# A two-layer encoder with expert retrieval: u blocks and gathered rows respaced, routing casts on ScalarE, gate scratch in groups of four blocks

## The chip, the core and the metric

One NeuronCore of a Trainium2 chip runs the whole kernel as one program. The metric is the device time of one execution in microseconds (us), lower being better. Engines are named as in the profile: PE is TensorE (matmuls; PEld its weight loads), DVE VectorE, ACT ScalarE, POOL GpSimd, SP SyncE, whose queue issues most loads.

## What is computed

Two residual layers over 512 tokens of width 1024: a mixer (convolution and windowed attention, or dense attention and spatial gating), then a retrieval layer over 16384 experts, and a last RMSNorm. The change lies in the retrieval layer alone:

```python
q = (ht @ wq).reshape(T, PEER_HEADS, 2, PEER_DKEY // 2)
s = jnp.einsum('thpd,hpkd->thpk', q, subkeys.astype(q.dtype)).astype(jnp.float32)
sv, si = lax.top_k(s, PEER_TOPK)
cand = (sv[:, :, 0, :, None] + sv[:, :, 1, None, :]).reshape(T, PEER_HEADS, PEER_TOPK * PEER_TOPK)
fv, fi = lax.top_k(cand, PEER_TOPK)
i1 = jnp.take_along_axis(si[:, :, 0, :], fi // PEER_TOPK, axis=-1)
i2 = jnp.take_along_axis(si[:, :, 1, :], fi % PEER_TOPK, axis=-1)
eidx = i1 * PEER_NKEYS + i2
gate = jax.nn.softmax(fv, axis=-1)
# for every token, over its 8 x 16 experts e: out += gelu(u[e] . x) * gate * v[e]
```

## The kernel before

The experts of a layer are 128 blocks of 128. For three of the four token tiles (384 tokens) the retrieval is done densely: a **u block** multiplies one block of `u` with all 384 tokens (24 matmuls `up` in three-term fp32r), ACT applies gelu (`A`), the result is multiplied with a gate matrix that is zero where an expert was not chosen, and a v block multiplies that with `v`. The fourth tile (GT) is done by gathering: a **row** is one gathered row of `u` or `v` per token (indirect DMA on POOL, tile `ug`) and one product on DVE; 256 rows per layer.

A u block takes a step of `u_step` (L1002): load of block b+3 on SP (`ur`, three buffers), rounding `uh` on ACT and remainder `ul` on DVE of block b+1 (two buffers each), gelu of the block before, matmuls of block b. While the routing is under way a block is **parked**: `A` is written to DRAM (`Ad`) and read back later (`Ar`). Blocks that are left when the routing ends are **fresh** and go straight into the combined stage of u and v blocks.

The routing is DVE's work: `topk` (L1101) finds the 16 best keys per head and half (an item is ten instructions for two halves), `route_top` (L1109) the 16 best sums, `route_rest` (L1227) the key numbers, by one-hot products and a `tree` of additions (L1206). `g_prep` and `g_build` (L1302, L1314) make one-hot matrices per token, PE multiplies them into the gate matrix (`gp`), ACT copies that to `stg`, and 12 writes of 2 MB per layer put it into DRAM scratch `Gd` (L1294); the combined stage reads it back as `G`, one read for four blocks (L1419).

All engines run in the order in which the program names their instructions; there is no scheduler. What sets the spacing is `tick` (L1044): each piece of routing work reports a cost in about microseconds of DVE, every `row_every` of it a row is put in, and every `u_every` (rows included at 1.15) a u block:

```python
            u_every, row_every = st["pace"]
            if st["rows"] and st["row"] < 2 * P:
                st["racc"] += cost
                while st["racc"] >= row_every and st["row"] < 2 * P:
                    st["racc"] -= row_every
                    row()
                    cost += 1.15
            st["acc"] += cost
            while st["acc"] >= u_every:
                st["acc"] -= u_every
                u_step()
```

PACE_T holds in the searches, PACE_R in the routes, PACE_G in the one-hot builds. Ahead of these stages stands the query loop (L1188), nine turns of query products, score products `sps`, and searches of tile GT and tile 0.

Of the kernel before, what the change touches and what calls it, by code (L numbers as in the profile page):

```python
# [10 lines left out]
F32 = mybir.dt.float32  # L11
# [9 lines left out]
P = 128  # L21
# [37 lines left out]
URB = 3  # L59
RAW1 = 2  # L60
RAWX = 8
AU = (8,)
LAST = 3
DGA = 3
F0 = 6
# [1 line left out]
AFILL = 2  # L67
QFILL = (2, 1)
CFILL = (3, 5, 4, 2)
PACE_T = (3.5, 3.7)  # L70
PACE_R = (3.5, 3.0)
PACE_G = (3.5, 3.0)
GSC = 4096.0
CSTART = [0, 16, 24, 29, 33, 36, 38, 40] + list(range(42, 50))
# [6 lines left out]
def trunk(ctx: ExitStack, tc: tile.TileContext, a: dict, out: bass.AP, stages=99):  # L81
# [3 lines left out]
    def pool(name, side):  # L85
        return tc.tile_pool(name=name, bufs=1, side=side, reuse_waits="tile")
# [864 lines left out]
    def peer(l, A, B):  # L951
# [2 lines left out]
        TG = ND * 4  # L954
        GT = NT - 1
        base = l * NK * NK
        Gd = tc.dram_tile([TG, P, NK, 32], F32, name=f"Gd{l}")
        Ad = [tc.dram_tile([P, SD], F32, name=f"Ad{l}_{b}") for b in range(NB)]
        ea, eb = ExitStack(), ExitStack()
        up = ea.enter_context(pool(f"ua{l}", A))  # L960
# [83 lines left out]
        def tick(cost):  # L1044
            if not st["pace"]:
                return
# [3 lines that stand above are left out]
                while st["racc"] >= row_every and st["row"] < 2 * P:  # L1050
                    st["racc"] -= row_every
                    row()
                    cost += 1.15
            st["acc"] += cost
            while st["acc"] >= u_every:
                st["acc"] -= u_every
                u_step()
# [43 lines left out]
        def topk(h, t, wkp):  # L1101
            xs = [2 * h, 2 * h + 1]
            srcs = [Ss[h][p][:, t, :] for p in range(2)]
            wks = [wkp.tile([P, NK], F32, tag="wk", bufs=4, name="wk") for _ in range(2)]
            top16(zip(xs, srcs, wks), sv[t], si[t])

        tops = {}

        def route_top(t, h0, h1, mid=None):  # L1109

            if t not in tops:
                tops[t] = [pl["a"].tile([P, NH, 16], dt, tag="f" + x, bufs=1, name="f" + x)
                           for x, dt in (("v", F32), ("i", U32))]
            hs, n = slice(h0, h1), h1 - h0
            c5 = pl["a"].tile([P, NH, NC50], F32, tag="c5", bufs=1, name="c5")[:, hs]
            v4 = sv[t].rearrange("p (h s) j -> p h s j", s=2)[:, hs]
            for j in range(8):
                m = 16 // (j + 1)
                nc.vector.tensor_tensor(c5[:, :, CSTART[j]:CSTART[j] + m], v4[:, :, 1, :m],
                                        v4[:, :, 0, j:j + 1].to_broadcast([P, n, m]), OP.add)  # L1120
            nc.vector.tensor_tensor(c5[:, :, 42:50], v4[:, :, 0, 8:16],
                                    v4[:, :, 1, 0:1].to_broadcast([P, n, 8]), OP.add)
            tick(1.2)
            if mid:
                mid()
            for h in range(0, n, 2):
                top16([(h0 + h + j, c5[:, h + j, :], pl["a"].tile([P, NC50], F32, tag="wk2", bufs=4, name="wk2"))
                       for j in range(2)], *tops[t])
                tick(1.25)

        pl["a"] = cs_.enter_context(pool(f"a3{l}", A))
        with pool(f"rq{l}", A) as qp:
            wraw, wspl, sps, qs = {}, {}, {}, {}

# [53 lines left out]
            for h in range(NH + 1):  # L1188
                w_load(h + 2)
                if h < NH:  # L1190
                    q_mm(h)
                if h:
                    s_mm(h - 1)
                    s_copy(h - 1)
                if h < NH:
                    q_split(h)
                w_split(h + 2)
                if h:
                    topk(h - 1, GT, qp)
                if h and h % RSTEP == 0:  # L1200
                    route_top(GT, h - RSTEP, h)
                elif h > 1:
                    topk(h - 2, 0, qp)
                if h in AU:
                    u_step()
        def tree(ms, extra=()):  # L1206
            extra = list(extra)
            n = 16
# [18 lines left out]
        def route_rest(t):  # L1227
# [8 lines left out]
            sf = pl["r"].tile([P, 2, 16, NH], F16, tag="sf", bufs=2, name="sf")  # L1236
            nc.vector.tensor_copy(sf.rearrange("p s j h -> p h s j"), si[t].rearrange("p (h s) j -> p h s j", s=2))
            dl = pl["r"].tile([P, 2, 16, NH], F16, tag="dl", bufs=2, name="dl")
            nc.vector.tensor_copy(dl[:, :, 0:1, :], sf[:, :, 0:1, :])
            nc.vector.tensor_sub(dl[:, :, 1:, :], sf[:, :, 1:, :], sf[:, :, :15, :])  # L1240
            fkf = fk.rearrange("p k h -> p (k h)")
            tick(1.3)

            def jkh(x):
                return x.rearrange("p j (k h) -> p j k h", h=NH)
# [4 lines left out]
            def oh(name):  # L1250
# [5 lines left out]
            nc.vector.tensor_tensor(jkh(m), jkh(ge), tab(dl[:, 0]), OP.mult)  # L1256
            m2 = oh("mk2")
            nc.vector.tensor_tensor(jkh(m2), jkh(ge), tab(diffT), OP.mult)
            tick(3.4)
            i1, sa = tree([m, m2])  # L1260
            bb = pl["r"].tile([P, 16, NH], F16, tag="bb", bufs=2, name="bb")
            nc.vector.tensor_sub(bb.rearrange("p k h -> p (k h)"), fkf, sa)
            nc.vector.tensor_copy(gt[:, 0].rearrange("p k h -> p (k h)"), i1)
            tick(2.6)
            ge2 = oh("ge2")
            nc.vector.tensor_tensor(jkh(ge2), bb[:, None].to_broadcast([P, 16, 16, NH]), tab(jT), OP.is_ge)
            m = oh("mk")
            nc.vector.tensor_tensor(jkh(m), jkh(ge2), tab(dl[:, 1]), OP.mult)
            gsum = sm.tile([P, NH], F32, tag="gsum", name="gsum")
            nc.vector.tensor_reduce(gsum, ga, AX.X, OP.add)  # L1270
            tick(3.5)
            i2 = tree([m], [lambda: nc.vector.reciprocal(gsum, gsum)])[0]
            nc.vector.tensor_copy(gt[:, 1].rearrange("p k h -> p (k h)"), i2)
            nc.vector.tensor_tensor(gt[:, 2].rearrange("p k h -> p h k"), ga,
                                    gsum.unsqueeze(2).to_broadcast([P, NH, 16]), OP.mult)
            tick(2.5)
            return gt.rearrange("p x k h -> p x (k h)")

        gq = []
# [1 line left out]
        def g_flush():  # L1281
            t, s, A2, Bh, Bl, stg = gq.pop(0)
            o = 16 * (s % 2)
            for q in range(4):
                gp = bank("v", [P, 4, NK], name="gp")
                for j in range(4):
                    tt = 4 * q + j
                    w, n = tt // TI, tt % TI
                    nc.tensor.matmul(gp[:, j, :], A2[:, w, :, n], Bh[:, w, :, n], start=True, stop=False)  # L1289
                    nc.tensor.matmul(gp[:, j, :], A2[:, w, :, n], Bl[:, w, :, n], start=False, stop=True)  # L1290
                nc.scalar.activation(stg[:, :, o + 4 * q:o + 4 * q + 4], gp.rearrange("p t i -> p i t"), AF.Copy,  # L1291
                                     scale=1.0 / GSC)
            if s % 2 == 1:
                nc.gpsimd.dma_start(Gd[t * 4 + s // 2], stg)  # L1294

        def g_transpose(gt):
            tp = bank("m", [P, 3, P], name="gtp")
# [1 line left out]
                nc.tensor.transpose(tp[:, j, :], gt[:, j, :], ident)  # L1299
            return tp  # L1300

        def g_prep(tp):  # L1302
            iT = pl["r"].tile([P, 2, P], F16, tag="iT", bufs=2, name="iT")
            nc.vector.tensor_copy(iT, tp[:, 0:2, :])
            g32 = pl["r"].tile([P, P], F32, tag="g32", bufs=2, name="g32")
            nc.vector.tensor_scalar(g32, tp[:, 2, :], GSC, None, OP.mult)
            gg = pl["r"].tile([P, 2, P], F16, tag="gg", bufs=2, name="gg")
            nc.vector.tensor_copy(gg[:, 0, :], g32)
            nc.vector.tensor_sub(gg[:, 1, :], g32, gg[:, 0, :])
            nc.vector.tensor_copy(g32, gg[:, 1, :])  # L1310
            tick(1.0)
            return iT, gg, g32

        def g_build(t, iT, gg, g32):  # L1314
# [45 lines left out]
                row_load()  # L1360

        def mid():
            hold["tp"] = g_transpose(hold["gt"])

        with pool(f"o3{l}", A) as pl["r"]:
            pl["oh"] = 3
# [13 lines left out]
        pl["r"] = pl["a"] = rt.enter_context(pool(f"ro{l}", A))  # L1380
# [31 lines left out]
        def v_load(i):  # L1412
# [242 lines left out]
```

## Time and profile before

| | us |
|---|---|
| median of 3 runs (lowest to highest) | 2888.75 (2886.06 to 2889.57) |
| the profiled execution | 2888.71 |
| its span, first to last instruction | 2886.6 |
| PE busy / DVE / ACT / POOL | 2788.8 / 2355.8 / 1220.9 / 765.8 |

In a layer the stages follow each other: the mixer, the query loop, the routing with its u blocks (layer 0 from 303 us, layer 1 from 1734), the combined stage (from 771 and 2199 us). PE's busy time counts matmuls in flight; the granted clock of a stretch is a share of 2.4 GHz, where time at the lower level counts as a half.

### The profile page before, as it was taken

Reading aid. Unit: us, or ns where it says so; the run is one execution under the profiler, and the core shown is the slowest. Engines: PE = TensorE matmul, PEld = TensorE weight load, DVE = VectorE, ACT = ScalarE, POOL = GpSimd, SP = SyncE. Lnnn points to the kernel's source line nnn. Section 1 sums busy time; section 2 is a strip of 40 time slices with the busy share of each in tenths; the row PEclk is TensorE's granted clock in tenths of the full one; section 3 lists DMA queues with packets and bytes.
Section 4 is the critical chain, followed back from the end, with each engine's and each line's share of the span. In section 5 each row is a group of like instructions: output and inputs, shape, how many; then the busy total and the mean of one; then the engine's idle time right before and its main releaser. Section 6 shows DMA issues by size and latency. Waiting matters only on the chain.

```text
span 2886.6 us, 43523 instructions
## 1 busy us (share of the span) xinstructions
PE 2788.8 (97%) x15844; PEld 2510.2 (87%) x15844; DVE 2355.8 (82%) x4692; ACT 1220.9 (42%) x2139; POOL 765.8 (27%) x730
## 2 busy tenths in 40 slices
PE   8999899999999999999999998899999999999998
PEld 7888789999999998888799888898999999888886
DVE  7866999888788887878777479998887888788887
ACT  4664324555533333333356333344564333333333
POOL 0000243333344442222100002343333444322220
PEclk9999999999999999999999999999999999999999
DMA  5102467889999999999812125677999999999995
GB/s 152 59 23 93 149 225 241 302 300 332 357 346 337 333 335 345 345 347 344 287 56 79 41 85 193 227 263 276 322 336 359 348 345 343 312 352 339 354 344 202
DMA packets 334343, 752.39 MB, mean 261 GB/s; under 512 B 27888, under 2 KB 184944, under 8 KB 331056
## 3 DMA queue, kind: packets, MB, share of 16 engines
q1 hardware_dynamic: 245424, 395.41, 40.5%
q0 software_dynamic: 88704, 354.20, 33.9%
q8 instruction: 124, 2.03, 0.3%
q14 instruction: 91, 0.75, 0.1%
HBM read 661.69 MB, written 87.82 MB: 260 GB/s over the span
## 4 chain that ended last, share of the span: by engine, by line
PE 79%; DVE 16%; ACT 2%; issue 2%; DMA 1%; SPq 0%; ACTq 0%; DVEq 0%
PE va L148 11%; PE va L146 11%; PE va L147 11%; PE up L148 9%; PE up L146 9%; PE up L147 9%; DVE ul L143 3%; DVE ug L1027 2%; PE gp L1289 1%; PE gp L1290 1%; PE O L417 1%; PE qp L146 1%; PE qp L147 1%; PE qp L148 1%; DVE wk L1064 1%
## 5 line engine op out<-in xcount | busy, mean ns | idle before, releaser
L148 PE MATMUL up<-hh,ul 128*128 128x384 f32 x2048 | 702.0, 343 | 46.5 <-DVE ul L143 46.3
L146 PE MATMUL up<-hh,uh 128*128 128x384 f32 x2048 | 702.2, 343 | 6.1 <-ACT A L990 5.6
L147 PE MATMUL up<-hl,uh 128*128 128x384 f32 x2048 | 696.8, 340 | 0.8 <-DVE hl L143 0.8
L146 PE MATMUL va<-vh,Wh 128*128 128x512 f32 x1536 | 600.7, 391 | 7.1 <-ACT Wh L1439 7.1
L148 PE MATMUL va<-vh,Wl 128*128 128x512 f32 x1536 | 600.3, 391 | 0.0
L147 PE MATMUL va<-vl,Wh 128*128 128x512 f32 x1536 | 599.3, 390 | 0.0
L142 ACT CAST uh<-ur 128x1024 fp32r<-128x1024 f32 x256 | 268.7, 1050 | 595.2 <-PE up L147 564.8
L1017 POOL DMA_INDIRECT ug<-in_peer_un,idx x256 | 354.3, 1384 | 614.9 <-DVE ug L1027 556.7
L1017 POOL DMA_INDIRECT ug<-in_peer_v,idx x256 | 296.4, 1158 | 680.8 <-DVE gacc L1036 633.4
L1438 ACT CAST vh<-vr 128x1024 fp32r<-128x1024 f32 x256 | 268.6, 1049 | 443.6 <-issue 283.3
L148 PEld LDWEIGHTS up<-hh,ul 128*128 128x128 f32 x2048 | 389.3, 190 | 61.8 <-DVE ul L143 61.5
L143 DVE TENSOR_TENSOR ul<-ur,uh 128x1024 fp32r<-128x1024 f32 x256 | 313.3, 1224 | 151.5 <-ACT uh L142 151.3
L1442 DVE TENSOR_TENSOR vl<-vr,vh 128x1024 fp32r<-128x1024 f32 x256 | 312.9, 1222 | 130.9 <-ACT vh L1438 130.7
L146 PEld LDWEIGHTS up<-hh,uh 128*128 128x128 f32 x2048 | 389.2, 190 | 11.8 <-ACT A L990 7.9
L147 PEld LDWEIGHTS up<-hl,uh 128*128 128x128 f32 x2048 | 389.1, 190 | 4.5 <-DVE hl L143 1.3
L146 PEld LDWEIGHTS va<-vh,Wh 128*128 128x128 f32 x1536 | 289.2, 188 | 65.1 <-ACT Wh L1439 7.9
L148 PEld LDWEIGHTS va<-vh,Wl 128*128 128x128 f32 x1536 | 289.1, 188 | 61.9 <-DVE Wl L1443 0.8
L147 PEld LDWEIGHTS va<-vl,Wh 128*128 128x128 f32 x1536 | 289.3, 188 | 59.0 <-DVE vl L1442 0.6
L1036 DVE SCALAR_TENSOR_TENSOR gacc<-ug,ag,gacc 128x1024 f32<-128x1024 f32 x254 | 325.2, 1280 | 3.9 <-DMA ug<-in_peer_v,idx 1.6
L1027 DVE SCALAR_TENSOR_TENSOR ug<-ug,hrow 128x1024 f32<-128x1024 f32 x256 | 306.0, 1218 | 0.0
L992 POOL DMA_DIRECT2D Ad<-A x180 | 101.6, 565 | 722.7 <-ACT A L990 720.7
L1291 ACT ACTIVATE stg<-gp 128x512 f32<-128x512 f32 x192 | 99.1, 603 | 136.8 <-PE gp L1290 136.8
(235 smaller groups left out, 3895.5 us busy)
## 6 DMA issues: line engine op xcount, KB each, us to landing
ur<-in_peer_u SPq DMA_DIRECT2D x256, 512.0 KB, 5.4
vr<-in_peer_v SPq DMA_DIRECT2D x256, 512.0 KB, 6.8
Gd<-stg POOLq DMA_DIRECT2D x24, 2048.0 KB, 8.5
G<-Gd SPq DMA_DIRECT2D x64, 768.0 KB, 8.9
Ad<-A POOLq DMA_DIRECT2D x180, 192.0 KB, 5.4
Ar<-Ad SPq DMA_DIRECT2D x180, 192.0 KB, 6.3
wqr<-in_peer_wq SPq DMA_DIRECT2D x16, 512.0 KB, 4.1
wr<-in_odd_w_in SPq DMA_DIRECT2D x28, 256.0 KB, 3.0
```

Source lines behind the costliest of these rows:

```text
L142: nc.scalar.copy(hi, src)
L143: nc.vector.tensor_sub(lo, src, hi.bitcast(F32))
L146: nc.tensor.matmul(out_, lh, rh, start=start, stop=False)
L147: nc.tensor.matmul(out_, lh, rl, start=False, stop=False)
L148: nc.tensor.matmul(out_, ll, rh, start=False, stop=stop)
L992: nc.gpsimd.dma_start(Ad[b], A)
L1017: nc.gpsimd.indirect_dma_start(out=rows[n], out_offset=None, in_=a["peer_un" if what == "u" else "peer_v"], in_offset=bass.IndirectOffsetO ...
L1027: nc.vector.scalar_tensor_tensor(x, x, 1.0, hrow, op0=OP.mult, op1=OP.mult, accum_out=a3[:, js])
L1036: nc.vector.scalar_tensor_tensor(gacc, x, ag[:, js], gacc, op0=OP.mult, op1=OP.add)
L1291: nc.scalar.activation(stg[:, :, o + 4 * q:o + 4 * q + 4], gp.rearrange("p t i -> p i t"), AF.Copy, scale=1.0 / GSC)
L1438: nc.scalar.copy(vh, raw)
L1442: nc.vector.tensor_sub(vl, raw, vh.bitcast(F32))
```

## The change

The pace is a block every 3.05 and a row every 2.1 in both PACE_T and PACE_R; the costs that are reported differ. In the query loop the block of the last turn becomes two, one ahead of the last score products and one behind them, and the route of GT ticks from there. `sf`, the key numbers as fp16, is made by ACT once per tile (`numbers`), as are the casts of the gate table for the dense tiles and of the transposed tables (`g_rows`). Three sums of `route_top` become one. `Gd` is laid out as [32 groups, 128, 12, 4 x 32], and written from ACT's queue.

```diff
-AU = (8,)
-PACE_T = (3.5, 3.7)
-PACE_R = (3.5, 3.0)
+PACE_T = (3.05, 2.1)
+PACE_R = (3.05, 2.1)
...
-        Gd = tc.dram_tile([TG, P, NK, 32], F32, name=f"Gd{l}")
+        Gd = tc.dram_tile([NK // SB, P, TG, SB * 32], F32, name=f"Gd{l}")
...
-                    cost += 1.15
+                    cost += 1.14
...
+        def numbers(t):
+            nc.scalar.copy(sfs[t].rearrange("p s j h -> p h s j"), si[t].rearrange("p (h s) j -> p h s j", s=2))
...
-            for j in range(8):
+            nc.vector.tensor_tensor(c5[:, :, CSTART[5]:CSTART[8]].rearrange("p h (j m) -> p h j m", m=2),
+                                    v4[:, :, 1, None, :2].to_broadcast([P, n, 3, 2]),
+                                    v4[:, :, 0, 5:8].unsqueeze(3).to_broadcast([P, n, 3, 2]), OP.add)
+            for j in range(5):
...
-            tick(1.2)
+            tick(0.8)
...
-                tick(1.25)
+                tick(1.58)
...
                 if h < NH:
                     q_mm(h)
+                else:
+                    u_step()
...
                 w_split(h + 2)
+                if h == NH:
+                    u_step()
                 if h:
                     topk(h - 1, GT, qp)
+                if h == NH:
+                    numbers(GT)
+                    st["pace"] = PACE_R
+                    tick(2.33)
...
-                if h in AU:
-                    u_step()
...
-            tick(1.3)
+            tick(0.65)
...
-            tick(3.4)
+            tick(3.53)
...
-            nc.vector.tensor_copy(gt[:, 0].rearrange("p k h -> p (k h)"), i1)
-            tick(2.6)
+            cast = nc.vector.tensor_copy if t == GT else nc.scalar.copy
+            cast(gt[:, 0].rearrange("p k h -> p (k h)"), i1)
+            tick(2.8)
...
-            tick(3.5)
+            tick(2.6)
...
-            tick(2.5)
+            tick(2.1)
...
-                nc.gpsimd.dma_start(Gd[t * 4 + s // 2], stg)
+                nc.scalar.dma_start(Gd[:, :, t * 4 + s // 2, :].rearrange("s p x -> p s x"),
+                                    stg.rearrange("p (s i) t -> p s (i t)", i=SB))
...
-        def g_prep(tp):
+        def g_rows(tp):
...
-            nc.vector.tensor_copy(iT, tp[:, 0:2, :])
+            nc.scalar.copy(iT, tp[:, 0:2, :])
...
-            nc.vector.tensor_scalar(g32, tp[:, 2, :], GSC, None, OP.mult)
+            nc.scalar.activation(g32, tp[:, 2, :], AF.Copy, scale=GSC)
...
-            nc.vector.tensor_copy(gg[:, 0, :], g32)
+            nc.scalar.copy(gg[:, 0, :], g32)
...
-            tick(1.0)
...
-            hold["tp"] = g_transpose(hold["gt"])
+            hold["tp"] = g_rows(g_transpose(hold["gt"]))
...
-                        tick(2.1)
+                        tick(2.33)
+                numbers(t)
...
-                nc.sync.dma_start(Gs[s], Gd[:, :, s * SB:(s + 1) * SB, :].rearrange("g p i t -> p g i t"))
+                nc.sync.dma_start(Gs[s].rearrange("p g i t -> p g (i t)"), Gd[s])
```

Line numbers move by -1 to +19. Three places in the order of the instructions: first ACT at the end of the query loop of layer 0, ahead of the exponential `ga` of tile GT (`qh` is the rounded query of the last head, `S` its two score copies). Before:

```order
L142 CAST qh<-qp 128x512
L1172 COPY S_2822<-sps 128x512
L1172 COPY S_2823<-sps 128x512
L142 CAST uh<-ur 128x1024
L990 ACTIVATE A<-up 128x384
L115 ACT_TABLE_LOAD
L1232 ACTIVATE ga<-ga 128x128
```

and of the change:

```order
L141 CAST qh<-qp 128x512
L141 CAST uh<-ur 128x1024
L989 ACTIVATE A<-up 128x384
L1179 COPY S_2822<-sps 128x512
L1179 COPY S_2823<-sps 128x512
L141 CAST uh<-ur 128x1024
L989 ACTIVATE A<-up 128x384
L1108 CAST sfg<-si_2801 128x8x32
```

A block stands ahead of the score copies now and one behind them; two further blocks come ahead of `ga`.

Second, DVE in the searches of tile 1 in layer 0 (the eight rows from `MAX` to `MAX_INDEX` are one item of ten instructions, `ug,a` is a row, `ul` the split of a u block). Before:

```order
L1027 SCALAR_TENSOR_TENSOR ug,a_2786<-ug,hrow 128x1024
L143 TENSOR_TENSOR ul<-ur,uh 128x1024
L1062 MAX sv_2795<-S_2814 128x8
L1062 MAX sv_2795<-S_2815 128x8
L1064 MATCH_REPLACE wk<-sv_2795,S_2814 128x128
L1064 MATCH_REPLACE wk<-sv_2795,S_2815 128x128
L1066 MAX_INDEX si_2799<-sv_2795,S_2814 128x8
L1066 MAX_INDEX si_2799<-sv_2795,S_2815 128x8
L1068 MAX sv_2795<-wk 128x8 x2
L1070 MAX_INDEX si_2799<-sv_2795,wk 128x8 x2
L1062 MAX sv_2795<-S_2816 128x8
L1062 MAX sv_2795<-S_2817 128x8
```

and of the change:

```order
L1026 SCALAR_TENSOR_TENSOR ug,a_2786<-ug,hrow 128x1024
L142 TENSOR_TENSOR ul<-ur,uh 128x1024
L1061 MAX sv_2795<-S_2810 128x8
L1061 MAX sv_2795<-S_2811 128x8
L1063 MATCH_REPLACE wk<-sv_2795,S_2810 128x128
L1063 MATCH_REPLACE wk<-sv_2795,S_2811 128x128
L1065 MAX_INDEX si_2799<-sv_2795,S_2810 128x8
L1065 MAX_INDEX si_2799<-sv_2795,S_2811 128x8
L1067 MAX sv_2795<-wk 128x8 x2
L1069 MAX_INDEX si_2799<-sv_2795,wk 128x8 x2
L1026 SCALAR_TENSOR_TENSOR ug,a_2786<-ug,hrow 128x1024
L142 TENSOR_TENSOR ul<-ur,uh 128x1024
```

Before, one item in four or five is followed by the next without a split; now nearly every item is followed by a row and a split.

Third, ACT in the one-hot builds of tile 0 (`stg` are four copies of the gate matrix, `Bl` four products for the next step). Before:

```order
L1291 ACTIVATE stg<-gp 128x128x4 x4
L1343 ACTIVATE Bl<-A_5598,g_5377 128x128 x4
L142 CAST uh<-ur 128x1024
L990 ACTIVATE A<-up 128x384
L142 CAST uh<-ur 128x1024
```

and of the change:

```order
L1304 ACTIVATE stg<-gp 128x128x4 x4
L1307 DMA Gd_2348<-stg 128x32x128
L1359 ACTIVATE Bl<-A_6115,g_5499 128x128 x4
L141 CAST uh<-ur 128x1024
L989 ACTIVATE A<-up 128x384
```

The write stands on ACT, between the copies and the rounding of the next block. On POOL it was one instruction over 128x4096.

## Rows read from the trace of the kernel before

**Rows 1.** Part 1 of the page: busy time, share of span, instructions.
```profile
PE 2788.8 (97%) x15844; PEld 2510.2 (87%) x15844; DVE 2355.8 (82%) x4692; ACT 1220.9 (42%) x2139; POOL 765.8 (27%) x730
```

**Rows 2.** Windows: length, busy time of PE, PEld, DVE, ACT, POOL; clock, DMA, GB/s.
```profile
303.40:338.00 34.60, 28.59 (x141) 27.61 (x141) 34.19 (x149) 12.37 (x17) 6.99 (x9) 0.90 0.36 118
338.00:435.00 97.00, 85.73 (x460) 83.43 (x459) 96.58 (x418) 29.12 (x41) 38.02 (x37) 0.96 0.73 243
435.00:598.00 163.00, 153.69 (x1002) 147.94 (x1001) 148.95 (x340) 75.73 (x133) 60.73 (x63) 1.00 0.78 268
598.00:750.00 152.00, 151.97 (x1221) 148.34 (x1220) 130.23 (x146) 91.65 (x189) 54.40 (x60) 1.00 0.90 329
1080.00:1395.00 315.00, 315.00 (x1392) 260.89 (x1391) 252.27 (x312) 115.07 (x157) 76.19 (x71) 1.00 0.98 342
1734.40:1769.00 34.60, 29.33 (x143) 28.66 (x143) 34.19 (x150) 12.17 (x17) 7.35 (x9) 0.86 0.37 118
1769.00:1866.00 97.00, 87.11 (x460) 84.54 (x458) 96.44 (x416) 29.34 (x41) 37.92 (x37) 0.95 0.73 245
1866.00:2028.00 162.00, 151.88 (x1000) 146.01 (x999) 148.81 (x339) 75.50 (x133) 61.23 (x63) 1.00 0.79 268
```

**Rows 3.** Waits of PE over the span: who for, total, times, longest.
```profile
PE up L148 <- DVE ul L143: 46.3, 36, 4.4
...
PE va L146 <- ACT Wh L1439: 7.1, 2, 4.7
PE up L146 <- ACT A L990: 5.6, 8, 1.1
PE sps L146 <- ACT qh L142: 3.3, 2, 1.6
```

**Rows 4.** Timeline of DVE in the searches: start, length, instruction, count.
```profile
343.90 1.20 DVE L1027 SCALAR_TENSOR_TENSOR ug<-ug,hrow 128x1024 f32<-128x1024 f32 x1
...
345.03 1.22 DVE L143 TENSOR_TENSOR ul<-ur,uh 128x1024 fp32r<-128x1024 f32 x1
346.17 0.48 DVE L1062 MAX8 sv<-S 128x8 f32<-128x128 f32 x2
...
348.52 1.21 DVE L143 TENSOR_TENSOR ul<-ur,uh 128x1024 fp32r<-128x1024 f32 x1
```

**Rows 5.** Timeline of ACT behind the last build, blocks without other work.
```profile
758.61 1.05 ACT L142 CAST uh<-ur 128x1024 fp32r<-128x1024 f32 x1 [2.80 <-PE up L147]
...
762.85 1.05 ACT L142 CAST uh<-ur 128x1024 fp32r<-128x1024 f32 x1 [2.80 <-PE up L147]
```

**Rows 6.** Timeline of DVE: two splits around the one-hot products of a route.
```profile
417.04 1.22 DVE L143 TENSOR_TENSOR ul<-ur,uh 128x1024 fp32r<-128x1024 f32 x1
...
424.41 1.22 DVE L143 TENSOR_TENSOR ul<-ur,uh 128x1024 fp32r<-128x1024 f32 x1
```

**Rows 7.** Timeline of ACT: an exponential of a route, and what stands behind it.
```profile
570.12 0.31 ACT L1232 ACTIVATE ga<-ga 128x128 f32<-128x128 f32 x1 [4.74 <-DVE ga L1230]
570.33 1.04 ACT L142 CAST uh<-ur 128x1024 fp32r<-128x1024 f32 x1
```

**Rows 8.** DMA issues of the page: count, KB each, median us to landing.
```profile
ur<-in_peer_u SPq DMA_DIRECT2D x256, 512.0 KB, 5.4
...
Gd<-stg POOLq DMA_DIRECT2D x24, 2048.0 KB, 8.5
G<-Gd SPq DMA_DIRECT2D x64, 768.0 KB, 8.9
```

**Rows 9.** Timeline of SP's queue at the start of the combined stage.
```profile
759.35 0.38 SPq L1419 DMA_DIRECT2D G<-Gd  x1
...
774.25 0.38 SPq L1419 DMA_DIRECT2D G<-Gd  x1
776.42 5.44 SPq L1421 DMA_DIRECT2D vr<-in_peer_v  x1
```

**Rows 10.** Timeline of ACT at that place: the first rounded gate product.
```profile
769.90 0.52 ACT L1439 CAST Wh<-W 128x384 fp32r<-128x384 f32 x1 [0.44 <-DVE W L1436]
```

**Rows 11.** Timeline of PE at that place: the first v matmul.
```profile
771.30 0.39 PE L146 MATMUL va<-vh,Wh 128*128 128x512 f32 x1
```

More of the change, by code (lines that the diff above doesn't have):

```diff
@@ L1092, in peer @@
         si = [sp_.tile([P, 16, 16], U32, name=f"si{t}") for t in range(NT)]
+        sfs = {}
         startT = sp_.tile([P, 16, NH], F16, name="startT")
@@ L1128, in route_top @@
                        for j in range(2)], *tops[t])
-                tick(1.25)
+                tick(1.58)
         pl["a"] = cs_.enter_context(pool(f"a3{l}", A))
+        sfs[GT] = pl["a"].tile([P, 2, 16, NH], F16, name="sfg")
         with pool(f"rq{l}", A) as qp:
@@ L1235, in route_rest @@
             nc.vector.tensor_copy(fk.rearrange("p k h -> p h k"), fi)
-            sf = pl["r"].tile([P, 2, 16, NH], F16, tag="sf", bufs=2, name="sf")
-            nc.vector.tensor_copy(sf.rearrange("p s j h -> p h s j"), si[t].rearrange("p (h s) j -> p h s j", s=2))
+            sf = sfs[t]
             dl = pl["r"].tile([P, 2, 16, NH], F16, tag="dl", bufs=2, name="dl")
@@ L1270, in route_rest @@
             nc.vector.tensor_reduce(gsum, ga, AX.X, OP.add)
-            tick(3.5)
+            tick(2.6)
             i2 = tree([m], [lambda: nc.vector.reciprocal(gsum, gsum)])[0]
-            nc.vector.tensor_copy(gt[:, 1].rearrange("p k h -> p (k h)"), i2)
+            cast(gt[:, 1].rearrange("p k h -> p (k h)"), i2)
             nc.vector.tensor_tensor(gt[:, 2].rearrange("p k h -> p h k"), ga,
                                     gsum.unsqueeze(2).to_broadcast([P, NH, 16]), OP.mult)
-            tick(2.5)
+            tick(2.1)
             return gt.rearrange("p x k h -> p x (k h)")
@@ L1300, in g_transpose, with g_prep @@
             return tp
-        def g_prep(tp):
+        def g_rows(tp):
             iT = pl["r"].tile([P, 2, P], F16, tag="iT", bufs=2, name="iT")
-            nc.vector.tensor_copy(iT, tp[:, 0:2, :])
+            nc.scalar.copy(iT, tp[:, 0:2, :])
             g32 = pl["r"].tile([P, P], F32, tag="g32", bufs=2, name="g32")
-            nc.vector.tensor_scalar(g32, tp[:, 2, :], GSC, None, OP.mult)
+            nc.scalar.activation(g32, tp[:, 2, :], AF.Copy, scale=GSC)
             gg = pl["r"].tile([P, 2, P], F16, tag="gg", bufs=2, name="gg")
-            nc.vector.tensor_copy(gg[:, 0, :], g32)
+            nc.scalar.copy(gg[:, 0, :], g32)
+            return iT, gg, g32
+        def g_prep(iT, gg, g32):
             nc.vector.tensor_sub(gg[:, 1, :], g32, gg[:, 0, :])
-            nc.vector.tensor_copy(g32, gg[:, 1, :])
-            tick(1.0)
+            nc.scalar.copy(g32, gg[:, 1, :])
             return iT, gg, g32
@@ L1370, in peer @@
         st["rows"] = True
+        sfp = rt.enter_context(pool(f"sf{l}", B))
+        sfs.update((t, sfp.tile([P, 2, 16, NH], F16, name=f"sf{t}")) for t in range(ND))
         st["pace"] = PACE_T
@@ L1389, in peer @@
                 mid()
-            iT, gg, g32 = g_prep(hold["tp"])
+            iT, gg, g32 = g_prep(*hold["tp"])
             if t + 1 < ND:
```

## The prediction

> **What bounds the kernel now.** I read the page first [rows 1]: TensorE (PE) is busy for 97% of the span, so only its idle time and its slow time can be won. The windows by stage [rows 2] say where these lie. While the routing runs without the one-hot builds (303.4 to 598 us of layer 0, 1734.4 to 2028 of layer 1) PE is idle for 34.6 - 28.59 = 6.0, 11.3 and 9.3 us in layer 0 and 5.3, 9.9 and 10.1 us in layer 1, 51.9 us in all; VectorE (DVE) is busy for 92 to 100% of each of these stretches, and in the first two the granted clock is below 1. From 598 us on PE is full, and in the combined stage (row 1080:1395) as well. The waits of PE [rows 3] name the cause: 46.3 us in 36 waits for the split `ul` on DVE, another 5.6 for the gelu on ScalarE (ACT), and 3.3 for `qh`. So in this stretch DVE hands over u blocks too seldom, or in lumps that are too long.
>
> **Part 1, the spacing (PACE_T, PACE_R and the ticks).** A u block costs PE 4.24 us: its casts on ACT start that far apart when nothing else is in the way [rows 5]. One search item of `topk` is 348.52 - 346.17 = 2.35 us on DVE, a row 345.03 - 343.90 = 1.13, a split 346.17 - 345.03 = 1.14 [rows 4]. Before, an item counts as 2.1 with a row every 3.7 and a block every 3.5. Per item that is 0.57 rows and (2.1 + 0.57 x 1.15) / 3.5 = 0.79 blocks, thus 2.35 + 0.64 + 0.90 = 3.89 us of DVE, or 4.9 us per block: DVE delivers one in 4.9 us and PE needs 4.24. Now an item counts as 2.33, a row is due every 2.1, a block every 3.05: 1.11 rows and (2.33 + 1.11 x 1.14) / 3.05 = 1.18 blocks per item, 2.35 + 1.25 + 1.35 = 4.95 us of DVE, 4.20 us per block. In `route` the ticks change by little in sum and the thresholds likewise, which gives 3.05 + 1.14 = 4.19. On average PE is just fed, and lumps remain.
>
> I priced these by going through the DVE order of layer 0 from split to split, with the durations of the rows. The rounding `uh` starts when PE has ended the block before last and `ul` is ready some 2.4 us later (1.05 + 1.22 and the hand-over), so 1.8 us before it is needed: an interval between splits passes unseen up to some 6.0 us, and longer ones make PE wait for the rest, as do runs of intervals over 4.24. For the order of before this count gives 30.5 us of waiting in a layer, where the rows show 46.3 / 2 = 23.2; it is a third too high, mostly since blocks at the slow clock swallow waits. For the new order it gives 9.9: three intervals of some 8 us (the start of a route: casts, differences and three one-hot products, with two rows and a split behind; the same piece with one row, and the `sf` cast in it, is 424.41 - 417.04 = 7.37 before [rows 6]), one of 7.4 behind the last dense tile's tree, and 1.9 us of drift in the searches. Scaled by 23.2 / 30.5 that leaves 7.5 us, 15 for both layers: **31 us gained**. Bounds: nothing left (46 gained) and the unscaled count with the rest of the stretch as it was (26).
>
> The clock: granted 0.90 and 0.96, 0.86 and 0.95 in the first two stretches of the layers. Time lost is window x (1 - clock): 3.5 + 3.9 + 4.8 + 4.9 = 17.1 us at most, less where PE idled anyway. Both low stretches are those with the long waits, and their waits of over 2 us fall from five to two or three per layer. I take half, **8 us**; ends 0 and 17.
>
> 14 more blocks per layer are parked (104, not 90; counted in the order): 14 more writes and reads of 192 KB, off PE. PE's own work is the same in all.
>
> **Part 2, the end of the query loop.** The first block of the burst now stands ahead of the last score products, and the second split ahead of the last search. PE's wait for `qh` (1.6 per layer) is covered by 4.24 us of u block: **3.3 us**. The 4.4 us wait for the third split goes too; it is in part 1. What is late next there is the exponential's `ga`, which holds ACT's queue (as in [rows 7]) as it does now.
>
> **Part 3, the casts on ACT.** `sf`, two gate casts per dense tile and four of the transposed tables leave DVE; the count above is made without them, so their gain is in it. On ACT a 128x128 piece costs 0.31 [rows 7], so the seven are some 2.5 us per tile on an engine busy for 30 to 46% there [rows 2]. They are not free all the same: ACT takes its queue in order, and the rounding `uh` of the next block stands behind `gt` casts that wait for DVE's tree and behind three copies that wait for PE's transposes. Such a copy group ends 0.4 + 0.9 us after the block before it; `uh` and `ul` follow with 2.4, which fits into 4.24 with 0.5 to spare. I count 0.35 us for each of the six cast pairs and six groups of both layers, **4 us lost**; bounds 0 (PE full anyway) and 12 x 1.05 = 13 (each costs a whole rounding). The Trainium skill has a rule that speaks against this part ("TensorE: Matmul & The Clock Gate", Architectural detail, on queue depths): the queues of ACT and DVE are strict FIFO. The trace agrees [rows 7]: ACT idled 4.74 us for `ga` with a rounding right behind. By the rule alone each cast costs its rounding, the upper end, and the time would be 2862.
>
> **Part 4, the scratch.** 24 writes of 2 MB go from POOL's queue, as 128 runs of 16 KB, to ACT's, as 4096 runs of 512 B (128x32x128 in the order), and 64 reads go the other way, from 512 B to 6 KB. A 2 MB write lands in 8.5 us now, a 768 KB read in 512 B runs in 8.9, 512 KB in 4 KB runs in 5.4 [rows 8]. So the write lands in 8.5 to 8.9 x 2.67 = 24 us afterwards, and the read in 5.4 to 8.9. The 152 us of 598:750 hold 16 steps, 9.5 us each [rows 2], and a staging buffer is wanted again three steps after its write, so the write hides there. Not at the end: the read of the first group waits for the last write (SP's queue issues it at 759.35, when that has landed), `Wh` is ready at 769.90 + 0.52, PE takes it up at 771.30 [rows 9, 10, 11]. The slack is 0.9 us. With a write of 12 us (nearer to its present row, since the last one meets little traffic) and a read of 7, the chain is 3.5 - 1.9 = 1.6 us longer; I take 1.5 per layer with the slow matmuls behind the wait, **3 us lost**; ends 0 and 2 x (15.5 - 0.9) = 29. By the Trainium skill ("DMA: Bandwidth & Descriptors", Specifications) 512 B is enough for line rate. The trace does not agree: the reads in such runs take longer than a write of 2.67 times the bytes [rows 8]. By the rule these 3 us would fall away, and the time be 2850.
>
> **Sum.** 31 + 8 + 3.3 - 4 - 3 = 35.3 us, off 2888.71 of the profiled execution (2886.6 of span, and 2.1 around it; its time is within 0.04 us of the median of the runs). That is **2853 us**.
>
> **Rivals.** (a) *Slower: the 4096-run writes block the load queue.* On SP a load issued behind a read of 1536 runs needs 5.44 us to issue, where that read itself took 0.38 [rows 9], so a transfer of many runs holds whatever is issued behind it. If ACT's and SP's issues share what is held, each write holds the `ur` loads 2.67 times as long, 13.6 us. The loads have three buffers: they are issued some 3 x 4.24 - 2.4 = 10.3 us ahead, and 5.4 of landing [rows 8] leaves 5. PE would then wait up to 8.6 us, 24 times: 206 us. From 1.5 us per write on (24 x 1.5 = 36) the gain is gone. Taking 3 us for a typical one, 72 - 35 gives 2925. For it: DMA is at 0.90 where the writes run. Against it: ACT itself has no other transfer behind, and nothing shows the two queues to be one. (b) *No change: the combined stage becomes DMA-bound.* There a v block takes 4.07 us (315 us, 1392 / 18 blocks) at 342 GB/s and a share of 0.98 [rows 2]. Fewer fresh blocks spread the remaining rows over it: 1.10 rows per v block instead of 0.93, 22 GB/s more, 4% above 342 / 0.98. That is 0.17 us x 98 blocks x 2 = 34 us, all of the gain: 2888. Against: the reads there come in longer runs now. (c) *Half:* the lumps keep two thirds of their waits and ACT costs its upper end: 46.3 / 3 + 5 + 3.3 - 9 = 15, 2874. (d) *All of it:* waits and clock vanish, 46 + 17 + 3 - 3: 2826. That the change fails to do what it says is excluded for the spacing: the order shows it.
>
> **How the numbers follow.** Forecast 0.52 (2838 to 2866), (c) 0.16, (d) 0.10, (b) 0.07, (a) 0.15. Faster by over 0.2% (5.8 us, about what a measurement of this kernel tells from no change) is forecast, (c) and (d): 0.78; within is (b): 0.07; slower is (a): 0.15. The range of 8 in 10 runs from 2828, which takes in most of (d), to 2884, the far end of (c); it leaves out (a) and most of (b).
>
> **What would show it.** Right: PE's wait for `ul` down from 46.3 to some 15 us with the three long intervals of a layer among what is left; a block every 4.2 to 4.4 us in the searches; clock over 0.97 there; no wait for `qh`; 104 parked blocks. Part 4: `Wh` at the start of the combined stage 1 to 3 us behind PE. Wrong: new waits of PE for `uh` behind ACT's copies; SP's `ur` issues of several us or DMA waits at `uh` beside the writes; PE below full after 598 us, or in the combined stage.

## The result, and the profile after

Measured: **2855.53 us** (median of 4 runs, 2854.59 to 2858.94) against 2888.91 us before (4 runs, 2886.06 to 2889.57); ratio 0.9888, 95% interval 0.9871 to 0.9906. The forecast was 2853 us in 2828 to 2884. The profiled execution took 2854.59 us with a span of 2852.8, 33.8 less than before.

Part 1 of the page of the changed kernel answers to [rows 1]:

```profile
PE 2775.6 (97%) x15844; PEld 2499.0 (88%) x15844; DVE 2337.4 (82%) x4628; ACT 1246.2 (44%) x2183; POOL 789.3 (28%) x734
```

PE idled 2886.6 - 2788.8 = 97.8 us before and idles 2852.8 - 2775.6 = 77.2 now: 20.6 us. The same 15844 matmuls take 13.2 us less, mostly by the clock: its mean over the span rose from 0.989 to 0.993, and span x (1 - clock) fell from 31.8 to 20.0. Together that is the whole gain. The waits of PE, to be read against [rows 3]:

```profile
PE up L147 <- DVE ul L142: 30.8, 24, 4.4
...
PE va L145 <- ACT Wh L1458: 6.2, 2, 4.9
...
PE up L145 <- ACT A L989: 2.0, 2, 1.1
```

The wait for `ul` fell by 15.5 us, not by 31, and its longest is 4.4 us as before. `qh` is gone from the list (3.3), as forecast; the gelu `A` gives 3.6 which the sum did not hold. The windows by stage, layer 0 and then the routing of layer 1 (columns as in [rows 2]):

```profile
298.40:333.30 34.90, 33.19 (x194) 32.55 (x193) 30.56 (x119) 16.85 (x23) 3.85 (x7) 0.95 0.41 132
333.30:440.00 106.70, 100.70 (x549) 98.40 (x548) 98.74 (x396) 37.02 (x50) 52.82 (x49) 0.97 0.82 272
440.00:532.00 92.00, 87.56 (x496) 86.88 (x495) 86.75 (x242) 39.00 (x61) 42.63 (x40) 1.00 0.81 273
532.00:600.00 68.00, 67.30 (x530) 65.50 (x529) 57.85 (x84) 40.83 (x86) 21.08 (x22) 1.00 0.91 297
600.00:630.00 30.00, 28.96 (x163) 28.33 (x162) 29.79 (x89) 13.35 (x18) 16.76 (x14) 1.00 0.87 289
630.00:793.00 163.00, 160.49 (x1258) 154.48 (x1257) 135.89 (x154) 95.51 (x197) 53.73 (x55) 1.00 0.95 320
...
1100.00:1360.00 260.00, 260.00 (x1148) 215.29 (x1148) 218.70 (x259) 94.38 (x128) 73.96 (x68) 1.00 0.98 365
...
1710.00:1743.00 33.00, 31.23 (x185) 30.54 (x183) 28.70 (x116) 16.83 (x23) 3.83 (x7) 0.95 0.40 132
1743.00:1845.00 102.00, 96.89 (x538) 94.70 (x537) 95.38 (x379) 34.39 (x47) 47.81 (x45) 0.98 0.81 274
```

PE idles 1.7 and 6.0 us in the first two, where [rows 2] has 6.0 and 11.3. The third stretch of [rows 2], with 9.3, answers to three here, from 440 to 630 us, with 4.4 + 0.7 + 1.0 = 6.2. Window x (1 - clock) in the low stretches is 1.7 + 3.2 + 1.7 + 2.0 = 8.6 us where it was 17.1. The combined stage runs at 365 GB/s with PE full: it was not DMA-bound at 342. One new thing shows behind the routing: 2.5 us idle in 630:793, where PE was full before (row 598:750 of [rows 2]); in layer 1 it is 2.9 (2040 to 2200 us). The prediction named this as a sign of being wrong. Most of it is not the scratch: 2.0 us are there without it (experiment 4) and 1.4 with the spacing alone (experiment 1).

Block by block, layer 0 loses 1.7 us for `ul` at block 3, **4.38 at block 10**, 1.3 at 31, 1.9 at 36, 2.55 at 46, 0.6 at 57, 1.0 at 69, 0.75 at 88, and the same in layer 1. Blocks 36, 46 and 69 are the three long intervals of the forecast. Block 10 is not: the count had 1.9 us for all of the searches. The timeline of DVE around it:

```profile
334.60 0.23 DVE L1373 CAST idx<-ef 128x128 int32<-128x128 f32 x1
...
337.02 0.29 DVE L1069 FIND_INDEX8 si<-sv,wk 128x8 uint32<-128x128 f32 x1
340.03 1.23 DVE L1026 SCALAR_TENSOR_TENSOR ug<-ug,hrow 128x1024 f32<-128x1024 f32 x1 [2.71 <-DMA ug<-in_peer_un,idx]
...
341.18 2.35 DVE L142 TENSOR_TENSOR ul<-ur,uh 128x1024 fp32r<-128x1024 f32 x2
```

and PE's behind it:

```profile
337.73 0.34 PE L146 MATMUL up<-hl,uh 128*128 128x384 f32 x1
342.45 0.69 PE L147 MATMUL up<-hh,ul 128*128 128x384 f32 x1 [4.38 <-DVE ul L142]
342.94 0.52 PE L145 MATMUL up<-hh,uh 128*128 128x384 f32 x1
...
347.64 0.34 PE L145 MATMUL up<-hh,uh 128*128 128x384 f32 x1
```

The indices are ready at 334.83, the first gather is issued at 335.72, and at 337.3 the account calls for its row: DVE stands still for 2.71 us with the splits of blocks 10 and 11 behind. After the wait PE's matmuls last 0.52 instead of 0.34 us until 347.4, which makes the block 2.5 us longer still. The group of the rows in the changed kernel, and the same group before, when a row was due every 3.7 (behind the bar: the idle time of DVE ahead of them and what ended it):

```profile
L1026 DVE SCALAR_TENSOR_TENSOR ug<-ug,hrow 128x1024 f32<-128x1024 f32 x256 | 306.7, 1218 | 5.2 <-DMA ug<-in_peer_un,idx 5.2
```

```profile
L1027 DVE SCALAR_TENSOR_TENSOR ug<-ug,hrow 128x1024 f32<-128x1024 f32 x256 | 306.0, 1218 | 0.0
```

### The profile page after: what moved, and what is told of

The parts are those of the page before. It is cut to its first block, busy times and chain, and to the rows that moved or that the text cites. A ratio compares the mean times of both kernels' runs of the same rounds, so it can differ in the third digit from the quotient of the medians.

```text
span 2852.8 us, 43744 instructions
## 1 busy us (share of the span) xinstructions
PE 2775.6 (97%) x15844; PEld 2499.0 (88%) x15844; DVE 2337.4 (82%) x4628; ACT 1246.2 (44%) x2183; POOL 789.3 (28%) x734
## 4 chain that ended last, share of the span: by engine, by line
PE 81%; DVE 11%; ACT 4%; DMA 2%; issue 1%; ACTq 0%; SPq 0%; DVEq 0%; POOLq 0%
PE va L147 12%; PE va L145 12%; PE va L146 12%; PE up L147 10%; PE up L145 10%; PE up L146 10%; DVE ul L142 3%; DVE ug L1026 2%; PE O L416 1%; ACT stg L1304 1%; PE qp L145 1%; PE qp L146 1%; PE qp L147 1%; PE gp L1302 1%; PE gp L1303 1%
## 5 line engine op out<-in xcount | busy, mean ns | idle before, releaser
L1016 POOL DMA_INDIRECT ug<-in_peer_un,idx x256 | 370.6, 1448 | 622.1 <-DVE ug L1026 577.5
L991 POOL DMA_DIRECT2D Ad<-A x208 | 118.1, 569 | 747.5 <-ACT A L989 739.0
L1458 ACT CAST Wh<-W 128x384 fp32r<-128x384 f32 x256 | 130.9, 511 | 63.9 <-DVE W L1455 63.6
```

Source lines behind the costliest of these rows:

```text
L991: nc.gpsimd.dma_start(Ad[b], A)
L1016: nc.gpsimd.indirect_dma_start(out=rows[n], out_offset=None, in_=a["peer_un" if what == "u" else "peer_v"], in_offset=bass.IndirectOffsetO ...
L1458: nc.scalar.copy(Wh, W)
```

## The experiments

The theory to test: the spacing makes the gain, casts and scratch matter little, and what is missing lies at block 10 and in the three long intervals. The rivals give the gain to DVE's relief by the casts, or to the scratch.

**1. The spacing alone** (before, with these, the other new ticks, the new places in the query loop and the merged sums of `route_top`):

```diff
-PACE_T = (3.5, 3.7)
-PACE_R = (3.5, 3.0)
+PACE_T = (3.05, 2.1)
+PACE_R = (3.05, 2.1)
...
-                        tick(2.1)
+                        tick(2.33)
```

> The kernel before with the spacing alone: the new paces, the new ticks and the new places of the blocks at the end of the query loop; the casts stay on DVE and the scratch stays as it was. Theory (the spacing makes the gain, the rest is within 5 us): about 2860 us, ratio 0.990, between 2854 and 2866; PE's wait for ul some 35 us, no wait for qh. Rival 1 (the gain is DVE's relief by the casts): 2876 or more, ul still over 40 us. Rival 2 (the scratch makes a good part of it, by the clock or the start of the combined stage): 2868 to 2875 with ul at some 31 us.

2862.65 us, ratio 0.9912 (0.9899 to 0.9926), `ul` 35.2 us, no wait for `qh`. The theory holds for this part: the spacing alone makes some 25 of the 33 us. Its longest wait, 5.3 us, is at block 10 too.

**2. The casts alone** (before, with `sf`, the gate casts and the transposed tables on ACT):

```diff
-            nc.vector.tensor_copy(gt[:, 0].rearrange("p k h -> p (k h)"), i1)
+            cast = nc.vector.tensor_copy if t == GT else nc.scalar.copy
+            cast(gt[:, 0].rearrange("p k h -> p (k h)"), i1)
...
-            nc.vector.tensor_copy(iT, tp[:, 0:2, :])
+            nc.scalar.copy(iT, tp[:, 0:2, :])
```

> The kernel before with the routing's casts on ACT alone; paces, ticks and scratch as before. Theory: the intervals in the routes shrink by some 0.7 us in each of the twelve routes, the searches stay as they were: 2880 to 2887 us, ratio 0.997 to 0.999. Rival 1 (DVE's relief makes the gain): 2870 or less. Rival 2 (the copies hold up the rounding on ACT, the prediction's 4 us and its bound of 13): 2890 to 2902, and new waits of PE for uh.

2885.17 us, ratio 0.9990 (0.9981 to 0.9999): 2 to 3 us, as the theory had. Its waits of PE:

```profile
PE up L148 <- DVE ul L143: 39.0, 38, 2.5
PE up L146 <- ACT A L990: 11.2, 13, 2.1
```

DVE's relief is there (46.3 to 39.0), but 5.6 of it comes back as a wait for the gelu on ACT. No wait for `uh` appears; where ACT holds something up, it is `A`.

**3. The scratch alone** (before, with layout and queue of the change):

```diff
-        Gd = tc.dram_tile([TG, P, NK, 32], F32, name=f"Gd{l}")
+        Gd = tc.dram_tile([NK // SB, P, TG, SB * 32], F32, name=f"Gd{l}")
...
-                nc.gpsimd.dma_start(Gd[t * 4 + s // 2], stg)
+                nc.scalar.dma_start(Gd[:, :, t * 4 + s // 2, :].rearrange("s p x -> p s x"),
+                                    stg.rearrange("p (s i) t -> p s (i t)", i=SB))
...
```

> The kernel before with the gates' scratch in groups of four and its writes on ACT's queue alone. Theory (the prediction's part 4): the last write lands later, 2892 us, between 2889 and 2897, with one longer wait of PE for Wh per layer. Rival 1 (no cost at all, as 512 bytes are long enough): 2888 to 2889, the wait for Wh unchanged. Rival 2 (the longer reads give something back in the combined stage): 2880 to 2885, with the wait for va on Wh of 7.1 us gone.

2899.27 us, ratio 1.0041 (1.0027 to 1.0054): 12 us lost, more than any theory had. Its DMA issues (count, KB, median us to landing; before in [rows 8]):

```profile
Gd<-stg ACTq DMA_DIRECT2D x24, 2048.0 KB, 13.6
G<-Gd SPq DMA_DIRECT2D x64, 768.0 KB, 7.8
```

These are medians. The chain of the prediction hangs on the last write of a layer and the first read: they took 12.4 and 4.6 us in layer 0, 14.9 and 4.7 in layer 1, where the prediction chose 12 and 7 (before: 8.1 and 6.5, 7.6 and 7.6). So the chain is 2.4 and 4.4 us longer, against a forecast of 1.6. That is not 12 us for both layers; a cost is missing.

**4. The scratch taken out of the change** (the changed kernel with the layout and the queue of before):

```diff
...
-                nc.scalar.dma_start(Gd[:, :, t * 4 + s // 2, :].rearrange("s p x -> p s x"),
-                                    stg.rearrange("p (s i) t -> p s (i t)", i=SB))
+                nc.gpsimd.dma_start(Gd[t * 4 + s // 2], stg)
...
```

> The changed kernel with the scratch as before (128 runs of 16 KB from POOL's queue, reads of 512 B runs); spacing and casts stay. Theory (the new scratch costs what it cost by itself, 12 us): 2842 to 2847 us, PE's wait for va on Wh down from 6.2 to 2 or less. Rival 1 (the prediction's 3 us, since more blocks are parked and the last write has cover): 2851 to 2854. Rival 2 (beside the new spacing the scratch pays, because the reads in the combined stage come in longer runs or POOL's queue is free): 2857 or more, a combined stage with PE under full.

2848.00 us, ratio 0.9859 (0.9844 to 0.9874): 7.5 us better than the changed kernel, 1 us short of the theory's range. The wait of PE for `Wh`, which was to fall to 2 us or less, is 5.1 (6.2 in the changed kernel): that part of the theory failed. With spacing and casts this kernel is also the partner of experiment 1: the casts, worth 2 to 3 us by themselves, are worth 2862.65 - 2848.00 = 14.6 us under the new spacing. There the interval ahead of block 36 is 7.66 us in place of 8.51, block 46 waits 2.55 in place of 3.3, and `A` stays at 2.1. In the profiled executions blocks 36, 46 and 69 together last 5.5 us less in each layer than in experiment 1; 2.5 (layer 0) and 2.7 us (layer 1) of it are wait, the rest slow matmuls behind the waits.

One place where the scratch costs shows on ACT. Two lots of `stg` copies in the changed kernel:

```profile
662.42 2.07 ACT L1304 ACTIVATE stg<-gp 128x512 f32<-128x512 f32 x4 [3.44 <-PE gp L1303]
664.52 0.37 ACTq L1307 DMA_DIRECT2D Gd<-stg  x1
664.93 1.32 ACT L1359 ACTIVATE Bl<-A,g 128x128 f16<-128x128 f16 x4 [0.44 <-DVE Bl L1356]
666.12 1.04 ACT L141 CAST uh<-ur 128x1024 fp32r<-128x1024 f32 x1
```

and the same place without the new scratch:

```profile
659.74 2.07 ACT L1304 ACTIVATE stg<-gp 128x512 f32<-128x512 f32 x4 [3.44 <-PE gp L1303]
661.66 1.33 ACT L1358 ACTIVATE Bl<-A,g 128x128 f16<-128x128 f16 x4
662.84 1.05 ACT L141 CAST uh<-ur 128x1024 fp32r<-128x1024 f32 x1
```

From the first `stg` copy to the rounding it is 3.70 us with the issue and 3.10 without, so `ul` and the block come late behind it: blocks 59, 75, 79 and 96 take 6.38 us instead of 6.05. The trace puts the 0.44 us ahead of `Bl` down to DVE; that the issue is behind it is what experiments 5 and 6 show, where these blocks take 6.05 us with the writes on POOL's queue and 6.34 with them on ACT's.

**5. and 6. Queue and layout apart.** The new layout from POOL's queue (edit of the changed kernel), and the old layout from ACT's (edit of the kernel of experiment 4):

```diff
-                nc.scalar.dma_start(Gd[:, :, t * 4 + s // 2, :].rearrange("s p x -> p s x"),
+                nc.gpsimd.dma_start(Gd[:, :, t * 4 + s // 2, :].rearrange("s p x -> p s x"),
```

> The changed kernel with the scratch in groups of four (4096 runs of 512 B for a write) and its writes back on POOL's queue. Theory (the short runs cost the 7 us that the kernel without the new scratch has gained): as the changed kernel, 2853 to 2858 us, a write lands in 13 us or more. Rival 1 (ACT's queue costs them): 2846 to 2850. Rival 2 (POOL makes 4096 descriptors itself and holds up the rows' gathers behind them): 2860 or more, new waits of DVE for ug or of PE for uh.

```diff
-                nc.gpsimd.dma_start(Gd[t * 4 + s // 2], stg)
+                nc.scalar.dma_start(Gd[t * 4 + s // 2], stg)
```

> The changed kernel with the scratch laid out as before (128 runs of 16 KB for a write, reads in 512 B runs), its writes on ACT's queue. Theory (the runs are what costs, the queue nothing): 2845 to 2850 us, a write lands in 8 to 9 us. Rival (the queue costs): 2853 to 2858 with the write at 8 to 9 us.

2852.91 and 2851.97 us, both 0.9873 (0.9858 to 0.9888). Both lie between the 0.9859 of experiment 4 and the 0.9888 of the change, and by time alone the intervals do not part them, and each time falls between the ranges of its theory and its rival. The PE timelines do. From the first matmul of block 50 to that of block 102 (the builds; layer 0, layer 1): 274.6 and 273.1 us in the changed kernel, 274.2 and 272.7 with ACT's queue alone, 271.4 and 269.7 with the layout alone, 271.4 and 269.9 with neither. From block 102 to the 121st v matmul (in the seventh v block): 61.3 and 62.8 in the changed kernel, 61.3 and 60.6 with the queue alone, 63.7 and 64.9 with the layout alone, 61.3 and 61.0 with neither. So **ACT's queue costs some 3 us per layer in the builds, and the layout 2.4 and 3.9 us at the start of the combined stage**, of which the changed kernel shows only 0 and 1.8. That PE comes there later is my reading of the difference, and no run tests it. The same two places hold the 12 us of experiment 3: against the kernel before, blocks 42 to 88, the builds there, are 2.5 and 2.9 us longer, and the stretch from block 88 to the sixth v block 1.4 and 5.0. Landing with the layout on POOL's queue, with the old layout on ACT's, and with the old layout on POOL's (experiment 4):

```profile
Gd<-stg POOLq DMA_DIRECT2D x24, 2048.0 KB, 12.3
```

```profile
Gd<-stg ACTq DMA_DIRECT2D x24, 2048.0 KB, 9.4
```

```profile
Gd<-stg POOLq DMA_DIRECT2D x24, 2048.0 KB, 8.4
```

It is the 512 B runs that make the write long, whichever queue issues it.

**7. The first row one item later** (changed kernel, one line at the release of the rows):

```diff
+            st["racc"] = -2.33
```

> The changed kernel with its first row put off by one search item (the rows' account starts at -2.33 where the rows are released). Theory (block 10's wait of 4.4 us per layer comes from a first row that is due before its gather has landed, and the slow matmuls behind it from that wait): PE's wait for ul down from 30.8 to some 22 us, 8.8 us from the waits and 2 to 5 from the clock, 2842 to 2846 us. Rival 1 (the interval there is DVE's own work, the gather is only what ended last): ul stays at 30 us and the time at 2853 to 2857. Rival 2 (the row that was put off lengthens a later interval by as much): ul 26 to 30, 2850 to 2855, with a new wait one block later.

2857.95 us, ratio 0.9889 (0.9874 to 0.9905): no gain. Block 10 waits 0.99 us instead of 4.38 and block 12 starts 5.3 us earlier, but every later row moved against the blocks: block 68 waits 3.15 with slow matmuls behind, others come up, 103 blocks are parked instead of 104, and at the start of the combined stage PE waits 2.5 and 2.8 us for `Wh` (0 and 1.3 in the changed kernel). My second rival has the kind of it, a later interval that grows, but not the figures: `ul` is 25.2 us, below its range, and the time above it.

**8. The first row alone left out of its place**, so that nothing else moves:

```diff
+        st["racc"] -= PACE_T[1]
+        st["acc"] += 1.14
```

> The changed kernel with its first row alone left out of its place (2.1 off the rows' account, 1.14 onto the blocks' account, so that all that follows keeps its place); that row is made up at the end. Theory (block 10 waits for the first row's gather; where the run with the late row lost it again, at block 68, was its shifted order): 4 us of wait at block 10 and 1 of slow clock per layer, 2843 to 2848 us, ul at some 23 us, the waits of blocks 31 to 88 unchanged. Rival (the time gained at block 10 is taken back later whatever the order, for another engine or DMA paces the parked part): 2853 to 2858.

2848.35 us, ratio 0.9859 (0.9842 to 0.9877): 7.2 us better than the change. Its DVE at that place:

```profile
336.02 0.28 DVE L1069 FIND_INDEX8 si<-sv,wk 128x8 uint32<-128x128 f32 x1
336.23 2.34 DVE L142 TENSOR_TENSOR ul<-ur,uh 128x1024 fp32r<-128x1024 f32 x2
```

The split follows at once, and block 10 waits 1.0 us instead of 4.38; block 12 starts 5.6 us earlier in layer 0 and 5.1 in layer 1, with the waits of blocks 31, 36 and 46 as they were (1.26, 1.88, 2.56). At block 102 6.0 and 3.3 us of that are left. That the gather was the cause of all but 1.0 us of the wait at block 10 is shown. `ul` is 25.5 us where I expected 23, and the wait for `Wh` rises from 6.2 to 9.1.

**9. The long tick of a route cut in three** (changed kernel):

```diff
+            tick(1.14)
             m = oh("mk")
             nc.vector.tensor_tensor(jkh(m), jkh(ge), tab(dl[:, 0]), OP.mult)
+            tick(1.26)
...
-            tick(3.53)
+            tick(1.13)
```

> The changed kernel with one tick of the routing cut in three: 1.14 behind the comparison, 1.26 behind the first product, 1.13 behind the second, in place of 3.53 behind all three (first row as in the changed kernel). Theory (the long intervals in the routes make PE wait): the count of the DVE order gives 7.1 in place of 9.9 us of waiting per layer, blocks 36, 46 and 69 lose 1.9, 2.6 and 1.0 us of wait and smaller ones come up behind them; about 25 us for ul in all, 2847 to 2851 us. Rival (waits there are swallowed or only moved): ul at 29 or more, 2854 to 2858.

2849.15 us, ratio 0.9858 (0.9843 to 0.9873): 6.4 us better, as counted. `ul` 23.6 us; blocks 36, 46 and 69 no longer wait, 38, 49 and 72 wait about 0.4.

**10. The three together** (experiments 4, 8 and 9 in one kernel).

> The changed kernel with all three: the tick cut in three, the first row left out of its place, the scratch as before. Theory (three separate terms that add): the sum of what the three gain by themselves, within 4 us; 2828 to 2836 if each does what its theory says. Rival (they share slack, as one wait covers another): less than two thirds of that sum, 2840 or more.

**2831.05 us, ratio 0.9800 (0.9787 to 0.9814)**: 24.5 us below the changed kernel, where the three by themselves sum to 7.5 + 7.2 + 6.4 = 21. They add.

```profile
PE up L147 <- DVE ul L142: 15.5, 27, 1.8
...
PE va L145 <- ACT Wh L1461: 7.1, 3, 5.5
```

**11. Other paces on top:**

```diff
-PACE_T = (3.05, 2.1)
-PACE_R = (3.05, 2.1)
+PACE_T = (2.9, 2.4)
+PACE_R = (2.95, 2.4)
```

> The kernel with all three (tick cut, first row left out of its place, old scratch) with other paces: blocks every 2.9 in the searches and 2.95 in the routes, rows every 2.4. Theory (the count of the DVE order: 2.9 in place of 5.9 us of waiting per layer): 2822 to 2827 us, ul at 10 us or less. Rival (the rows that are left over crowd the combined stage, or the blocks come so early that parking takes their gain): 2829 to 2836.

2830.79 us, ratio 0.9804 (0.9791 to 0.9818): no better. Its waits:

```profile
PE up L147 <- DVE ul L142: 9.3, 19, 1.8
...
PE up L145 <- ACT A L989: 5.7, 5, 1.6
```

`ul` falls as counted, by 6.2 us, and `A` rises by what ACT then holds up; layer 0 is 5.0 us ahead of experiment 10 at block 40, 0.6 at block 90, and 2 behind at its last v block. The rival has the time. I have not separated what took back the rest.

## Why the prediction was right, and where its steps were not

- **The total** was 2 us off, and that it came so near is luck: the errors cancel. In the trace the 33.8 us are `ul` 15.5, `A` 3.6, `qh` 3.3, `Wh` 0.9, other waits -2.7, and PE's busy time 13.2. The sum had 31 for `ul`, 8 for the clock, 3.3, nothing for `A`, and -7 for casts and scratch. So `ul` fell 15.5 short. PE's busy time gave 5.2 more than the clock term, `A` and `Wh` 4.5 that the sum did not hold, other waits took 2.7; and the 7 us of losses have no row of their own, what they cost is already in these rows.
- **Part 1, `ul`: 31 forecast, 15.5 measured.** The mechanism is right: experiment 1 has it by itself, and the named intervals are where the waits are. The size failed at two steps. Scaling the count by 23.2 / 30.5 was wrong: without blocks 3 and 10 a layer waits 9.3 us, where the unscaled count without its searches has 9.9 - 1.9 = 8.0. And the count took a row to cost its 1.14 us on DVE alone. A row needs its gather; with a row due after the first item it is not there (5.2 us of DVE in both layers, 4.4 of PE's waiting in each), and the 1.7 at block 3 was taken as gone.
- **The clock: 8 forecast; 8.5 in the stretches named** (17.1 to 8.6), 13.2 in PE's whole busy time. Some of what is left stands behind the long waits: 2.5 us in block 10. The sign of over 0.97 in the searches was met in layer 1 (0.98) and just missed in layer 0 (0.97). The block every 4.2 to 4.4 us there (4.3 from block 12 to block 30) and the 104 parked blocks came as forecast.
- **Part 2, `qh`: 3.3 forecast, 3.3 measured.** The third split's wait fell from 4.4 to 1.7, not to nothing.
- **Part 3, the casts: 4 us of loss forecast, 1.3 found, and not where it was looked for.** PE never waits for `uh`. But in the builds ahead of block 88 DVE waits for ACT's copy `gg`, and the split behind it comes late; with the casts on ACT block 88 waits 0.75 us in each layer and lasts 0.64 longer (experiment 4 against experiment 1):

```profile
715.10 0.29 DVE L1326 TENSOR_TENSOR gg<-g,gg 128x128 f16<-128x128 f32 x1 [1.74 <-ACT gg L1322]
```

- Experiment 2 shows a loss under the old spacing, at the gelu (5.6 us). With DVE's relief, which the prediction had within part 1, the casts gain 14.6 us under the new spacing. By the strict queue order that the Trainium skill states ("TensorE: Matmul & The Clock Gate", Architectural detail) they were to cost the upper end, 13 us. The trace agrees with that order where I did not look, at a DMA issue in ACT's queue (0.37 us, and the rounding 0.6 us later).
- **Part 4, the scratch: 3 us forecast, 7.5 measured in the change, 12 by itself.** "Hides in the builds" is the step that failed: I priced the transfer and not the issue, which takes ACT 0.37 us 24 times with a rounding behind it. The queue makes some 3 of the 3.2 us that a layer's builds lose. The landing time was nearly right (12 chosen, 12.4 and 14.9 for the last writes of experiment 3), and the start of the combined stage cost 0 and 1.8 us in the change (the sign, `Wh` 1 to 3 us behind PE, came in layer 1 alone, with 1.3). By the Trainium skill ("DMA: Bandwidth & Descriptors", Specifications) 512 B is enough for line rate; the runs speak against it, 12.3 us for 2 MB in 512 B runs and 8.4 in 16 KB runs from the same queue.
- **Rivals.** (a) is refuted by the issues of `ur` and of the writes in the changed kernel (ns: shortest, median, longest; start of first and last): the longest on SP is 0.57 us, so ACT's transfers do not hold SP's.

```profile
L967 SPq DMA_DIRECT2D ur<-in_peer_u x256: 327/328/572, 176.1 to 2375.7; - x128
```

```profile
L1307 ACTq DMA_DIRECT2D Gd<-stg x24: 366/366/383, 548.4 to 2202.4; - x24
```

- (b) is refuted by the 365 GB/s. (c), 2874, was 18 us off, (d), 2826, 30. But (c) has the size of part 1: two thirds of the waits for `ul` kept is 46.3 / 3 = 15.4 gained, and 15.5 were; it is its other terms that failed. It also takes 9 us off where the upper end of part 3 is 13; with 13 its time would be 2878. Experiment 10 comes within 5 us of (d), with 15.5 us of `ul` left and without the new scratch, so not by the way of (d).

## What to carry to other kernels

A table of paces is priced by walking the order of the engine that delivers, but each item in that order has its own inputs: check for every work item that was moved earlier when its gather or load can be there. A pace changed in one place shifts everything behind it; to try a single step, put the account back so that the rest stays where it is. Count the issue of a DMA as an instruction of the queue that issues it, with all that stands behind.

## What the runs showed of the hardware

- A DMA issue on ACT took 0.37 us in all of 24 cases, and at the place shown the rounding behind it came 0.6 us later.
- 2 MB in 4096 runs of 512 B landed in 12.3 to 14.9 us over five kernels (medians); in 128 runs of 16 KB in 8.3 to 9.4 over seven, whichever of two queues issued it.
- A first gather of 128 rows reached its reader 4.3 us after its issue.
- After 4.38 us without work PE ran some 4.5 us of matmuls at 0.52 us each in place of 0.34, and then returned; the granted clock of 342.4 to 347.4 us is 0.50, the lower level. Behind shorter waits it differs: in experiment 1 block 69 waited 1.9 us in both layers, and 11 of its matmuls were slow in layer 0, none in layer 1.
